# Feed-forward up projection by Strassen's seven block products, with the gated values through DRAM

## The chip, the cores and the metric

The kernel runs on one core of a Trainium2 chip. The metric is the device time of one execution in microseconds (us), as the median over runs.

## What is computed

A backbone of two layers works on 1024 latent tokens and 256 context tokens of 1024 features, all in float32. Each layer has a mixer (attention, long convolution, linear attention), an output projection, and a feed-forward part with 2816 hidden features:

```python
def swiglu(u, w1, w3, w2):
    return (jax.nn.silu(u @ w1) * (u @ w3)) @ w2

h_lat = h_lat + g1_l * merge_heads(attn_l, hy_out_l, gla_out_l, r_l, out_norm_g, w_out)
h_lat = h_lat + g2_l * swiglu(modulate(rms_norm(h_lat, norm2_g), sh2_l, sc2_l), ffn_w1, ffn_w3, ffn_w2)
if update_ctx:      # layer 0 only
    h_ctx = h_ctx + g1_c * merge_heads(...)
    h_ctx = h_ctx + g2_c * swiglu(modulate(rms_norm(h_ctx, norm2_g), sh2_c, sc2_c), ffn_w1, ffn_w3, ffn_w2)
```

The modulation vectors (`sh2`, `sc2`, `g2` and their like) are products of a conditioning vector with `ada_w`. In layer 1 the context is no longer updated.

## The kernel before

Features lie on partitions and tokens along the free axis. Tokens come in blocks `BLK`: block 0 and block 1 of 512 latent tokens, block 2 of 256 context tokens. Every float32 operand of a matmul is split into a high and a low part (`split`: ScalarE copies the rounded high part, GpSimd subtracts it and writes the low part), and `mm3` makes one product of three matmuls: high by high, high by low, low by high. All matmuls of the program have the line of `mm`, L175; every low part has the line of `lo`, L187; every high part that is a plain copy has L421.

`phase34` holds the part that changes. In order: the output projection `w_out` (block 0, then blocks 1 and 2, the residual `h` staying in SBUF); norm 2 (`square` sums the squares, `spread` brings the reciprocal root of each token to all partitions through a matmul with `ones`, `norm_u` scales, shifts and splits into `u`); then the feed-forward part over 22 chunks of 128 hidden features, taken in pairs `m0`, `m0 + 1`. For each chunk `hidden(m, b)` makes the two products of `u` with `ffn_w1` and `ffn_w3` for a block (2 x 8 x 3 matmuls), gates them (L1497, L1498) and splits the gated value into `g` (L1499, L187), which stays in SBUF. After the two chunks of a pair, the down projection adds eight products for each block to `h` (L1537), six matmuls each. The last pair also makes the squares for the norm that follows.

`ada_dve` makes half a modulation vector on VectorE (16 instructions, L327 and L329, over rows of `ada_w` streamed into the tile `nsq`); `ada_next` starts the next of them and closes the one before with four wide and four narrow float32 matmuls.

Order: the program is written in program order, and a planner then fixes each engine's order ahead of the run. It issues on each engine, as it expects times, the ready instruction that stands earliest in program order. In the run each engine goes through its fixed list and stops at the first instruction whose operands are not there. All DMAs named here are issued by SyncE (SP), also in a fixed list. Tiles of one tag share a few buffers; a new tile of the tag waits until the last reader of the old one is done. Pools that are closed give their room to pools opened later, and each new tile there waits for the readers of the old tiles that lay at its place (`reuse_waits="tile"`).

## Time and profile before

| | |
|---|---|
| runs | 3711.64, 3715.42, 3720.87 us; median 3715.42 us |
| the profiled execution, first to last instruction | 3712.2 us |
| PE busy | 3563.2 us, 96% of the span, 17903 matmuls |
| VectorE (DVE) busy | 2014.1 us, 54% |
| GpSimd (POOL) busy | 1353.5 us, 36% |
| ScalarE (ACT) busy | 1088.0 us, 29% |
| feed-forward part of layer 0 | about 1102 to 2072 us of the span |
| feed-forward part of layer 1 | about 2964 us to the end |
| DMA | 310.63 MB, 84 GB/s over the span |

The profile is one execution. Its own time is given as its span of 3712.2 us; no separate time of that execution stands around it, and the median of the runs lies 3.2 us above it. Times in its rows are microseconds from the start of the span; PE is TensorE's matmuls, PEld its weight loads. A row's idle time names the engine that ended it.

### The profile page before, as it was taken

What the parts mean: (1) busy time and instruction counts of PE and PEld (TensorE: products, weight loads), DVE (VectorE), ACT (ScalarE), POOL (GpSimd) and SP (SyncE); (2) the same over time, 40 slices, a digit from 0 to 9 for tenths busy, and PEclk for the clock granted to TensorE, in tenths of its full rate; (3) what the DMA queues carried; (4) which work ended last, traced back from release to release, by engine and by line L of the source; (5) the groups of instructions that cost most, each with busy time, mean ns of one, the idle gap of its engine ahead of it and who ended that gap; (6) DMA issues with size and microseconds to landing.
All of it is one profiled execution on the core that took longest, in us unless ns stands there. A gap on an engine that the chain in (4) does not pass through costs nothing.

```text
span 3712.2 us, 46254 instructions
## 1 busy us (share of the span) xinstructions
PE 3563.2 (96%) x17903; PEld 2693.5 (73%) x17903; DVE 2014.1 (54%) x3271; ACT 1088.0 (29%) x1956; POOL 1353.5 (36%) x960
## 2 busy tenths in 40 slices
PE   8999899999999999999999899899999999999999
PEld 4789845445677888888888688865445788888887
DVE  6755667863677665644223773757753533223233
ACT  4243233553422111111111333333554421111112
POOL 2424564664333111111111541656764542221221
PEclk9999999999999999999999899999999999999999
DMA  9333311120633323321111333411112421111111
GB/s 329 99 124 123 120 33 43 56 81 20 212 110 99 95 80 89 90 66 54 49 35 46 107 111 116 150 49 42 35 70 71 139 63 51 40 57 46 52 40 57
DMA packets 275804, 310.63 MB, mean 84 GB/s; under 512 B 18680, under 2 KB 205727, under 8 KB 274304
## 3 DMA queue, kind: packets, MB, share of 16 engines
q1 hardware_dynamic: 269279, 287.75, 24.6%
q0 software_dynamic: 2560, 13.89, 1.0%
q10 hardware_dynamic: 3744, 6.03, 0.4%
q8 instruction: 140, 2.29, 0.3%
q14 instruction: 81, 0.66, 0.1%
HBM read 245.75 MB, written 61.87 MB: 83 GB/s over the span
## 4 chain that ended last, share of the span: by engine, by line
PE 75%; DVE 11%; POOL 4%; issue 3%; DMA 3%; ACT 1%; SPq 0%; DVEq 0%; POOLq 0%; ACTq 0%
PE ps L175 74%; PE ps L184 1%; POOL hss L928 1%; DMA nsq<-in_ada_w 1%; POOL hl L187 1%; DVE acc L329 1%; DVE mx L1032 1%; DVE sg L1138 1%; DMA yr<-y_d 0%; DVE h L1537 0%; POOL hy L936 0%; DVE sg L1150 0%; DVE sg L1151 0%; DVE nacc L365 0%; DVE hx L930 0%
## 5 line engine op out<-in xcount | busy, mean ns | idle before, releaser
L175 PE MATMUL ps<-u,hl 128*128 128x512 f32 (+1 forms) x6504 | 1384.4, 372 | 20.6 <-DVE u L403 6.2
L175 PEld LDWEIGHTS ps<-u,hl 128*128 128x128 f32 x6504 | 1136.3, 190 | 252.5 <-issue 14.9
L187 POOL TENSOR_TENSOR hl<-raw,hl 128x1024 fp32r<-128x1024 f32 x148 | 366.5, 2479 | 944.3 <-ACT hl L421 924.5
L175 PE MATMUL ps<-g,w 128*128 128x512 f32 (+1 forms) x2688 | 556.6, 367 | 10.0 <-DVE h L1537 3.4
L175 PEld LDWEIGHTS ps<-g,w 128*128 128x128 f32 x2688 | 466.6, 190 | 95.5 <-DVE h L1537 5.4
L1068 POOL TENSOR_TENSOR ac<-ac,p 128x512 f32<-128x512 f32 x256 | 354.7, 1394 | 159.4 <-ACT p L1057 158.8
L1498 DVE TENSOR_TENSOR s<-ps,s 128x512 f32<-128x512 f32 (+1 forms) x110 | 70.0, 637 | 614.7 <-PE ps L175 597.3
L1537 DVE SCALAR_TENSOR_TENSOR h<-ps,mod,h 128x512 f32<-128x512 f32 (+1 forms) x448 | 303.5, 687 | 181.8 <-PE ps L175 181.6
L175 PE MATMUL ps<-p,V 128*64 128x512 f32 x672 | 309.8, 607 | 4.7 <-ACT p L1057 2.5
L187 POOL TENSOR_TENSOR w<-raw,w 128x1024 fp32r<-128x1024 f32 x44 | 109.0, 2477 | 500.0 <-ACT w L421 499.9
L1032 DVE TENSOR_REDUCE mx<-ps 128x1 f32<-128x512 f32 (+1 forms) x400 | 221.0, 587 | 120.8 <-PE ps L175 119.8
L1057 ACT ACTIVATE p<-ps 128x512 f32<-128x512 f32 (+1 forms) x336 | 194.6, 586 | 286.8 <-PE ps L175 277.7
L175 PEld LDWEIGHTS ps<-Q,K 65*128 65x128 f32 (+1 forms) x672 | 105.0, 191 | 222.2 <-issue 209.8
L421 ACT CAST hl<-raw 128x1024 fp32r<-128x1024 f32 x148 | 154.9, 1049 | 303.9 <-PE ps L175 151.5
L329 DVE SCALAR_TENSOR_TENSOR acc<-nsq,silc,acc 128x512 f32<-128x512 f32 x252 | 210.6, 876 | 61.3 <-DMA nsq<-in_ada_w 60.6
L175 PE MATMUL ps<-Q,K 65*128 65x512 f32 (+1 forms) x672 | 242.2, 442 | 1.2 <-ACT p L1057 1.1
L175 PE MATMUL ps<-y,hl 128*128 128x512 f32 (+1 forms) x960 | 213.8, 381 | 13.2 <-DVE y L187 6.1
L175 PEld LDWEIGHTS ps<-y,hl 128*128 128x128 f32 x960 | 170.8, 194 | 59.3 <-DVE y L187 8.2
L421 ACT CAST w<-raw 128x1024 fp32r<-128x1024 f32 x44 | 46.2, 1051 | 491.8 <-PE ps L175 443.2
L175 PE MATMUL ps<-my,dft 128*128 128x256 f32 (+1 forms) x1176 | 166.8, 294 | 10.3 <-DVE my L187 9.7
L1499 ACT CAST g<-s 128x512 fp32r<-128x512 f32 (+1 forms) x110 | 63.3, 576 | 385.2 <-DVE s L1498 385.2
L175 PEld LDWEIGHTS ps<-my,dft 128*128 128x128 f32 x1176 | 159.1, 203 | 20.6 <-DVE my L187 13.7
(265 smaller groups left out, 4129.2 us busy)
## 6 DMA issues: line engine op xcount, KB each, us to landing
raw<-in_ffn_w SPq DMA_DIRECT2D x132, 512.0 KB
nsq<-in_ada_w SPq DMA_DIRECT2D x144, 256.0 KB
raw<-in_w_in SPq DMA_DIRECT2D x36, 512.0 KB
raw<-in_w_out SPq DMA_DIRECT2D x32, 512.0 KB
ada<-in_ada_w SPq DMA_DIRECT2D x24, 512.0 KB
h_d<-h SPq DMA_DIRECT2D x32, 256.0 KB
dft<-in_c_dft POOLq DMA_DIRECT2D x8, 1024.0 KB, 7.2
qd<-qT_d SPq DMA_DIRECT2D x64, 128.0 KB
```

The costliest lines, as they stand in the source:

```text
L175: self.nc.tensor.matmul(out, w, x, start=start, stop=stop)
L184: self.nc.tensor.transpose(out, in_, self.ident[:n, :n])
L187: eng.tensor_tensor(out=out, in0=x, in1=hi.bitcast(F32), op=ALU.subtract)
L329: nc.vector.scalar_tensor_tensor(out=acc[w], in0=raw, scalar=s, in1=acc[w], op0=ALU.mult, op1=ALU.add)
L421: self.nc.scalar.copy(hi, raw)
L928: nc.gpsimd.tensor_tensor(out=ss, in0=ss, in1=self.mh[:, :nh], op=ALU.pow)
L1032: nc.vector.tensor_reduce(out=mx[:, j, i:i + 1], in_=pm, op=ALU.max, axis=AX.X)
L1057: nc.scalar.activation(p, st, AF.Exp)
L1068: nc.gpsimd.tensor_tensor(out=acc[j], in0=x, in1=ps[j], op=ALU.add)
L1498: nc.vector.tensor_tensor(out=s, in0=p3, in1=s, op=ALU.mult)
L1499: nc.scalar.copy(gs[m][:, 0, o:o + n], s)
L1537: nc.vector.scalar_tensor_tensor(out=h, in0=ps, scalar=self.mod[l][:, 40 + k, w:w + 1], in1=h, op0=ALU.mult, op1=ALU.add)
```

## The change

The up projection of the 1024 latent tokens is no longer made chunk by chunk. Two chunks of hidden features by two halves of the 1024 input features form a 2 x 2 matrix of weight blocks (`A11` to `A22`), and two halves of the features by the two token blocks form a 2 x 2 matrix of activations (`B11` to `B22`). The method `up` takes, for each pair of chunks and each of the two weight matrices, seven block products of four `mm3` each instead of eight. Four of the seven use sums of weight blocks (`S1` to `S4`, VectorE), which are split on the fly; four use sums of activation blocks (`T1` to `T4`), which the new method `norm_sums` makes once for each layer in place of block 1's norm, on VectorE, ScalarE and GpSimd. Partial sums are copied out of PSUM between products and the same bank is added to further. The context tokens (layer 0) keep their eight products a weight matrix and chunk.

The gated values of all 22 chunks go to DRAM (`g_d`), and the down projection becomes a second phase that loads them back, splits them (ScalarE and GpSimd) and uses them. `h` leaves SBUF for the duration of `up`: `w_out` stores each piece to `h_d`, and the down phase loads it again. The `ada` work is spread over the pairs of `up`.

```diff
+        usc = self.pool("us", 1, reuse_waits="tile")
+        us = usc.__enter__()
+        B = {n: self.t(us, [P, 2, 4, 512], F32R, n) for n in ("T3", "T4", "B22", "T1", "T2")}
+        B["B11"], B["B21"] = u[0][:, :, 0:4], u[0][:, :, 4:8]
+        for b in blks[1:]:
+            for k in range(KC):
+                r[b] = self.square(self.h[b], k, BLK[b][1], aux, r.get(b))
+            if b == 2:
+                norm2(2, us)
+            else:
+                self.norm_sums(B, a[:, :, 0], self.mod[l][:, 24:32, 0], self.spread(r[0], 512, aux), self.spread(r[1], 512, aux), aux)
+        self.hpool.__exit__(None, None, None)
+        with self.pool("up", 1, side="right", reuse_waits="tile") as wp:
+            self.up(l, B, u.get(2), wp, ada_next, 0 if last else 14)
+        usc.__exit__(None, None, None)
...
+            for b in blks:
+                o, n = BLK[b]
                 for k in range(KC):
+                    nc.sync.dma_start(out=self.h[b][:, k, :], in_=self.h_d[k][:, o:o + n])
...
             for m0 in range(0, NHC, 2):
+                for m in (m0, m0 + 1):
+                    raw = self.t((self.wp, wp)[m % 2], [P, KC, P], F32, "raw", 1)
                     nc.sync.dma_start(out=raw.rearrange("p a b -> p (a b)"), in_=A["ffn_w2"][l][m * P:(m + 1) * P, :])
+                    if m % 3 < 2:
+                        w2s[m] = self.hl[:, m % 3 * 2048:m % 3 * 2048 + 2048].rearrange("p (s k c) -> p s k c", s=2, k=KC)
+                    else:
+                        w2s[m] = self.t(wp, [P, 2, KC, P], F32R, "w2", 1)
                     self.split(raw, w2s[m][:, 0], w2s[m][:, 1])
+                    raw = self.t(gp, [P, nt], F32, "graw", 2 if last else 1)
+                    nc.sync.dma_start(out=raw, in_=self.g_d[m][:, :nt])
+                    gs[m] = self.t(gp, [P, 2, nt], F32R, "g", 3)
+                    self.split(raw, gs[m][:, 0], gs[m][:, 1])
...
+    def norm_sums(self, B, scale, shift, r0, r1, tp):
+        def block(b, k, r):
+            x = self.t(tp, [P, 512], F32, ("s", "acc")[b], 2)
+            nc.vector.scalar_tensor_tensor(out=x, in0=self.h[b][:, k, :], scalar=scale[:, k:k + 1], in1=r, op0=ALU.mult, op1=ALU.mult)
+            nc.scalar.activation(x, x, AF.Identity, bias=shift[:, k:k + 1])
+            return x
+
+        def out(name, k, x, eng):
+            self.split(x, B[name][:, 0, k], B[name][:, 1, k], eng)
+
+        for k in range(4):
+            b12, b11 = block(1, k, r1), block(0, k, r0)
+            nc.gpsimd.tensor_tensor(out=b11, in0=b12, in1=b11, op=ALU.subtract)
+            out("T1", k, b11, nc.vector)
+            b22 = block(1, k + 4, r1)
+            nc.gpsimd.tensor_tensor(out=b12, in0=b22, in1=b12, op=ALU.subtract)
+            out("T3", k, b12, nc.gpsimd)
+            out("B22", k, b22, nc.vector)
+            b21 = block(0, k + 4, r0)
+            nc.gpsimd.tensor_tensor(out=b11, in0=b22, in1=b11, op=ALU.subtract)
+            out("T2", k, b11, nc.vector)
+            nc.gpsimd.tensor_tensor(out=b21, in0=b21, in1=b11, op=ALU.subtract)
+            out("T4", k, b21, nc.gpsimd)
+
+    def up(self, l, B, uc, wp, ada_next, nada):
+        nc, A = self.nc, self.A
+        self.roles((6,), (7,), (0,), (1,), (2,), (3,), (4, 5))
+        self.cyc = (6,)
+        extra = 2 if uc is not None else 5
+        nring = 0
+        def ring():
+            nonlocal nring
+            i = nring % (4 + extra)
+            nring += 1
+            if i < 4:
+                return self.hl[:, i * 1024:(i + 1) * 1024].rearrange("p (s k c) -> p s k c", s=2, k=4)
+            return self.t(wp, [P, 2, 4, P], F32R, "hs", extra)
+        def parts(a):
+            x = ring()
+            self.split(a, x[:, 0], x[:, 1])
+            return x
+        def tile(n=512, tag="c", bufs=6):
+            return self.t(wp, [P, 512], F32, tag, bufs)[:, :n]
+        def product(ps, a, b, start, more=False):
+            for k in range(4):
+                self.mm3(ps, (a[:, 0, k], a[:, 1, k]), (b[:, 0, k], b[:, 1, k]), start and k == 0, k == 3, skip_group_check=True)
+        def store(m, b, g):
+            o, n = BLK[b]
+            nc.sync.dma_start(out=self.g_d[m][:, o:o + n], in_=g)
+        def gated(m, b, x, y):
+            nc.scalar.activation(x, x, AF.Silu)
+            nc.vector.tensor_tensor(out=x, in0=x, in1=y, op=ALU.mult)
+            store(m, b, x)
+        for p in range(0, NHC, 2):
+            W = []
+            for src in (A["ffn_w1"], A["ffn_w3"]):
+                raws = []
+                for i in range(2):
+                    raw = self.t((self.wp, wp)[min(len(W) + i, 1)], [P, KC, P], F32, "raw", 3 if len(W) + i else 1)
+                    nc.sync.dma_start(out=raw, in_=src[l][:, (p + i) * P:(p + i + 1) * P].rearrange("(k p) c -> p k c", p=P))
+                    raws.append(raw)
+                W.append({"A11": raws[0][:, 0:4], "A12": raws[0][:, 4:8], "A21": raws[1][:, 0:4], "A22": raws[1][:, 4:8]})
+            def summed(w, out, x, y, op):
+                z = tile(512, "S", 4).rearrange("p (k c) -> p k c", k=4)
+                nc.vector.tensor_tensor(out=z, in0=W[w][x], in1=W[w][y], op=op)
+                W[w][out] = z
+            a, d, s1, s2, s5 = ([None, None] for _ in range(5))
+            hl = [{}, {}]
+            for w in range(2):
+                bk = self.ps(3 * w + 1)
+                hl[w]["A12"] = parts(W[w]["A12"])
+                product(bk, hl[w]["A12"], B["B21"], True)
+                hl[w]["A11"] = parts(W[w]["A11"])
+                a[w] = self.ps(3 * w)
+                product(a[w], hl[w]["A11"], B["B11"], True)
+                s1[w] = tile()
+                nc.scalar.copy(s1[w], a[w])
+                nc.vector.tensor_tensor(out=s1[w], in0=bk, in1=s1[w], op=ALU.add)
+            gated(p, 0, s1[0], s1[1])
+            def context(m, x, y):
+                if uc is None:
+                    return
+                ps = []
+                for w in range(2):
+                    ps.append(self.ps()[:, :NCTX])
+                    for k in range(KC):
+                        v = hl[w][x if k < 4 else y]
+                        self.mm3(ps[w], (v[:, 0, k % 4], v[:, 1, k % 4]), (uc[:, 0, k], uc[:, 1, k]), k == 0, k == KC - 1)
+                g = tile(NCTX)
+                nc.scalar.activation(g, ps[0], AF.Silu)
+                nc.vector.tensor_tensor(out=g, in0=ps[1], in1=g, op=ALU.mult)
+                store(m, 2, g)
+            context(p, "A11", "A12")
+            for w in range(2):
+                summed(w, "S1", "A21", "A22", ALU.add)
+                d[w] = self.ps(3 * w + 2)
+                product(d[w], parts(W[w]["S1"]), B["T1"], True)
+                s5[w] = tile()
+                nc.scalar.copy(s5[w], d[w])
+            for w in range(2):
+                summed(w, "S2", "S1", "A11", ALU.subtract)
+                product(a[w], parts(W[w]["S2"]), B["T2"], False)
+                s2[w] = tile()
+                nc.scalar.copy(s2[w], a[w])
+            for w in range(2):
+                summed(w, "S4", "A12", "S2", ALU.subtract)
+                product(d[w], parts(W[w]["S4"]), B["B22"], False)
+                nc.vector.tensor_tensor(out=s2[w], in0=d[w], in1=s2[w], op=ALU.add)
+            gated(p, 1, s2[0], s2[1])
+            for w in range(2):
+                summed(w, "S3", "A11", "A21", ALU.subtract)
+                product(a[w], parts(W[w]["S3"]), B["T3"], False)
+                nc.vector.tensor_tensor(out=s5[w], in0=a[w], in1=s5[w], op=ALU.add)
+            gated(p + 1, 1, s5[0], s5[1])
+            for w in range(2):
+                hl[w]["A22"] = parts(W[w]["A22"])
+                product(a[w], hl[w]["A22"], B["T4"], False)
+            g = tile()
+            nc.scalar.activation(g, a[0], AF.Silu)
+            nc.vector.tensor_tensor(out=g, in0=a[1], in1=g, op=ALU.mult)
+            store(p + 1, 0, g)
+            if uc is not None:
+                for w in range(2):
+                    hl[w]["A21"] = parts(W[w]["A21"])
+                context(p + 1, "A21", "A22")
+            for _ in range(2 if p < 6 else 1 if nada else 0):
+                ada_next()
...
     def w_out(self, l, blks, ys, yp):
...
+                nc.sync.dma_start(out=self.h_d[m][:, BLK[b][0]:BLK[b][0] + n], in_=h)
```

## Rows read from the trace of the kernel before

**Rows 1.** The page: busy time of PE, then the chain that ended last, by engine.

```profile
PE 3563.2 (96%) x17903; PEld 2693.5 (73%) x17903; DVE 2014.1 (54%) x3271; ACT 1088.0 (29%) x1956; POOL 1353.5 (36%) x960
...
PE 75%; DVE 11%; POOL 4%; issue 3%; DMA 3%; ACT 1%; SPq 0%; DVEq 0%; POOLq 0%; ACTq 0%
```

**Rows 2.** Stage windows: busy time and instructions of each engine, clock, DMA share, GB/s.

```profile
1232.00:1822.00 590.00, 590.00 (x3066) 496.44 (x3065) 311.60 (x432) 91.41 (x135) 102.53 (x42) 1.00 0.25 75
...
2985.00:3690.00 705.00, 703.44 (x3160) 584.35 (x3160) 223.22 (x283) 125.72 (x170) 158.63 (x69) 1.00 0.16 48
```

**Rows 3.** Groups by shape, 2985 to 3690 us: busy time, mean ns, idle before.

```profile
L175 PE MATMUL ps<-u,hl 128*128 128x512 f32 x2033 | 463.1, 389 | 0.2 <-POOL u L187 0.2
...
L1537 DVE SCALAR_TENSOR_TENSOR h<-ps,mod,h 128x512 f32<-128x512 f32 x168 | 124.9, 749 | 80.5 <-PE ps L175 80.5
L187 POOL TENSOR_TENSOR hl<-raw,hl 128x1024 fp32r<-128x1024 f32 x41 | 98.5, 2405 | 310.1 <-ACT hl L421 310.1
...
L421 ACT CAST hl<-raw 128x1024 fp32r<-128x1024 f32 x41 | 43.1, 1052 | 127.5 <-issue 70.1 <-PE ps L175 55.7 <-DMA raw<-in_ffn_w 1.7
```

**Rows 4.** Groups by shape, 1232 to 1822 us: narrow matmuls, those of ada.

```profile
L175 PE MATMUL ps<-u,hl 128*128 128x256 f32 x672 | 83.9, 283 | 0.0
...
L175 PE MATMUL ps<-acc,ones 128*64 128x512 f32 x44 | 16.1, 618 | 0.0
```

**Rows 5.** Windows of the tile hl alone, at both starts of the feed-forward part.

```profile
1102.00:1143.00 41.00, 30.33 (x108) 21.80 (x106) 2.07 (x2) 5.18 (x2) 0.83 0.21 61
...
2964.00:2985.30 21.30, 19.45 (x82) 14.96 (x81) 2.11 (x2) 5.19 (x2) 1.00 0.41 121
```

**Rows 6.** Timeline at both starts: block 1's root spread, its first scaled chunk.

```profile
1119.57 1.02 PE L175 MATMUL ps<-nsq,ones 128*128 128x512 f32 x2
...
2979.46 0.75 DVE L397 SCALAR_TENSOR_TENSOR s<-h,nsc,ps 128x512 f32<-128x512 f32 x1 [4.66 <-PE ps L175]
...
2985.30 15.75 PE L175 MATMUL ps<-u,hl 128*128 128x512 f32 x68 [0.17 <-POOL u L187]
```

**Rows 7.** Timeline of one norm, layer 1: scale, shift, high copy, low part.

```profile
2946.17 0.74 DVE L397 SCALAR_TENSOR_TENSOR acc<-h,nsc,ps 128x512 f32<-128x512 f32 x1
2946.28 0.73 ACT L402 ACTIVATE u<-s,mod 128x512 fp32r<-128x512 f32 x1 [0.68 <-DVE s L397]
...
2950.00 1.30 POOL L187 TENSOR_TENSOR u<-acc,u 128x512 fp32r<-128x512 f32 x1
2950.44 0.61 ACT L421 CAST u<-acc 128x512 fp32r<-128x512 f32 x1
```

**Rows 8.** Timeline: VectorE subtractions or sums of 512 columns, alone and beside GpSimd.

```profile
1417.96 1.42 DVE L329 SCALAR_TENSOR_TENSOR acc<-nsq,silc,acc 128x512 f32<-128x512 f32 x2 [0.60 <-DMA nsq<-in_ada_w]
...
1419.29 0.68 DVE L187 TENSOR_TENSOR g<-s,g 128x512 fp32r<-128x512 f32 x1
...
1419.89 8.36 DVE L329 SCALAR_TENSOR_TENSOR acc<-nsq,silc,acc 128x512 f32<-128x512 f32 x6
1419.94 2.95 POOL L187 TENSOR_TENSOR hl<-raw,hl 128x1024 fp32r<-128x1024 f32 x1 [27.31 <-ACT hl L421]
...
1423.98 2.40 POOL L187 TENSOR_TENSOR hl<-raw,hl 128x1024 fp32r<-128x1024 f32 x1 [1.09 <-ACT hl L421]
```

**Rows 9.** Windows of the start of layer 0's output projection (columns as in rows 2).

```profile
964.00:968.00 4.00, 1.44 (x3) 1.16 (x4) 4.00 (x9) 1.97 (x5) 0.63 (x1) 0.58 0.96 289
968.00:972.00 4.00, 4.00 (x12) 3.04 (x10) 4.00 (x6) 2.28 (x3) 2.58 (x1) 0.57 0.87 269
...
990.00:996.00 6.00, 6.00 (x26) 4.32 (x24) 3.55 (x6) 2.22 (x3) 2.39 (x1) 1.00 1.09 353
```

**Rows 10.** Landing of DMAs that write or read the DRAM tensor y_d (from its tile view).

```profile
DMA to landing us min/median/max: 2.0/3.7/6.2
```

More of the change, by code (lines that the diff above doesn't have):

```diff
@@ L171, in act_table, with mm, mm3 @@
         self.epoch.__enter__()
-    def mm(self, out, w, x, start, stop):
-        self.nc.tensor.matmul(out, w, x, start=start, stop=stop)
-    def mm3(self, out, w, x, start, stop):
-        self.mm(out, w[0], x[0], start, False)
-        self.mm(out, w[0], x[1], False, False)
-        self.mm(out, w[1], x[0], False, stop)
+    def mm(self, out, w, x, start, stop, **kw):
+        self.nc.tensor.matmul(out, w, x, start=start, stop=stop, **kw)
+    def mm3(self, out, w, x, start, stop, **kw):
+        self.mm(out, w[0], x[0], start, False, **kw)
+        self.mm(out, w[0], x[1], False, False, **kw)
+        self.mm(out, w[1], x[0], False, stop, **kw)
     def tr(self, out, in_, n=P):
@@ L1456, in phase34 @@
             yc.__exit__(None, None, None)
-        with ExitStack() as es:
-            self.upc = self.pool("u", reuse_waits="tile")
-            up = self.upc.__enter__()
-            if last:
-                es.push(self.upc)
-            wp = es.enter_context(self.pool("w4", 1, reuse_waits="tile"))
-            weights = {}
-            def load(m):
-                c = slice(m * P, (m + 1) * P)
-                ws = []
-                for i, src in enumerate((A["ffn_w1"], A["ffn_w3"])):
-                    j = 2 * m + i
-                    ws.append(self.load_w(src[l][:, c], wp=wp if j % 3 == 2 else None, raws=wp if i else None))
-                weights[m] = ws
-            load(0)
-            for b in blks[1:]:
+        nt = NLAT if last else NTOK
@@ new lines, in phase34 @@
+        usc = self.pool("us", 1, reuse_waits="tile")
+        us = usc.__enter__()
+        B = {n: self.t(us, [P, 2, 4, 512], F32R, n) for n in ("T3", "T4", "B22", "T1", "T2")}
+        B["B11"], B["B21"] = u[0][:, :, 0:4], u[0][:, :, 4:8]
+        if not last:
+            ada = [(l, 5, i) for i in range(2)] + [(l + 1, p, i) for p in range(6) for i in range(2)]
+        for b in blks[1:]:
[5 more added lines that the diff above has]
+                self.norm_sums(B, a[:, :, 0], self.mod[l][:, 24:32, 0], self.spread(r[0], 512, aux), self.spread(r[1], 512, aux), aux)
@@ L1502, in phase34 @@
             for m0 in range(0, NHC, 2):
                 end = m0 == NHC - 2
-                for m in range(m0, m0 + 2):
-                    if m not in weights:
-                        load(m)
-                    ws[m] = weights.pop(m)
-                    gs[m] = self.t(gp, [P, 2, nt], F32R, "g")
-                    raw = self.t(wp, [P, KC, P], F32, "raw", 1)
+                w2s, gs = {}, {}
+                for m in (m0, m0 + 1):
+                    raw = self.t((self.wp, wp)[m % 2], [P, KC, P], F32, "raw", 1)
@@ L1526, in phase34 @@
                     w, r = 0 if b < 2 else 1, None
-                    if end and not last:
-                        hidden(NHC - 1, b)
-                        if norm1:
+                    for k in range(KC):
+                        if k == 2 and norm1:
                             self.norm1(l + 1, *norm1, up)
-                    for k in range(KC):
+                            norm1 = None
                         ps = self.ps()[:, :n]
@@ L1544, in phase34 @@
                         norm1 = b, self.spread(r, n, aux)
-                for _ in range(2 if m0 < 8 else 1):
+                if m0 < 8:
                     ada_next()
```

40 lines of the change are left out of this document (14 added, 26 removed).

## The prediction

> **What bounds the kernel now.** I read the page first, then the chain, then windows over the two feed-forward parts, then groups by shape, then the timeline at the places where the change cuts in. The page says that PE is busy for 96% of the span and the chain runs through PE for 75% of it [rows 1]: time is saved by giving PE less to do, and lost wherever PE is made to stand. The windows sharpen this: from 1232 to 1822 us PE is busy for 590.0 of 590 us, in layer 1 from 2985 to 3690 us for 703.4 of 705, at full clock [rows 2]. There the other engines wait for PE. So each matmul taken out is worth its full length, 463.1 / 2033 = 0.228 us for 512 columns [rows 3] and 83.9 / 672 = 0.125 us for 256 [rows 4], and each new stop costs its full length. All that the change can lose is in its seams: the start of the up phase, the passage to the down phase, and the joints between pairs there.
>
> **Products.** A pair of chunks took 2 chunks x 2 weights x 2 blocks x 24 = 192 wide matmuls for the latent tokens; seven products of 12 for two weights are 168. 24 fewer, times 11 pairs, times 2 layers, is 528, times 0.228 us: **-120 us**. Context and down matmuls stay. Inside a pair I charge nothing. Each product lasts 12 x 0.228 = 2.7 us and needs one split of 512 columns: 0.61 us on ScalarE, 1.30 on GpSimd [rows 7]. GpSimd's 14 splits take 18 of the 38 us of PE in layer 1, 16 take 21 of 50 in layer 0 (with 96 narrow matmuls), and the ring of nine or six places lets them run ahead. A bank that is copied out is used again only after at least one other product, 2.7 us, against a copy of some 0.7. Without that cover each of 308 products would wait; the point is priced below. Stores of gated values wait in SP's list, with the next pair's weight loads behind them, but those have about 20 us of room.
>
> VectorE is the nearest to its limit, in layer 0's first three pairs, which carry two `ada` halves each. Its instructions that read and write SBUF stretch beside GpSimd: six sums took 8.36 us, against 1.42 for two alone, while two GpSimd subtractions ran [rows 8]. If the two exclude each other, such a pair needs 21 on GpSimd, 11 x 0.68 = 7.5 for sums and gates and 32 x 0.71 = 22.7 for `ada`: 51 us, against PE's 38.3 + 12.0 + about 3.8 for `ada`'s wide and narrow matmuls (16.1 / 44 = 0.37 us a wide one [rows 4]) = 54. Covered, barely: **0**, between -5 (layer 0's present first pair stands a few us for `ada` too) and +10.
>
> **The start of the up phase.** Today PE goes from the output projection into `hidden` of block 0, whose `u` has long been made, while block 1's norm runs. It does 108 matmuls (some eight of them narrow) from 1102 to 1143 us, and 82 from 2964.0 to 2985.3 [rows 5], and then never stops. After the change only the four products on `B11` and `B21` (48 matmuls, 10.9 us) can run before the `T` sums. Those need block 1's root, which comes at about 1120 and 2979.5 us [rows 6].
>
> `norm_sums` then goes through four steps. A step has on GpSimd four subtractions and two low parts, 6 x 1.30 = 7.8 us, but the temporaries have two buffers a block, and one chain returns to the same buffer: first subtraction 1.3; its high copy 0.6; its low part on VectorE, shut out by GpSimd's second subtraction, to 3.3; T3's low part and B22's take their turns, to 5.3; third subtraction, 6.6; high copy, 7.3; its low part, shut out again by the fourth subtraction, 8.6; then the buffer is free for scale 0.74 and shift 0.73 [rows 7], with handovers 10.3 us. So T1 is whole after 3 x 10.3 + 2.3 + 3.3 = 36 us, T4 after 43. In layer 1 PE goes on at 36. In layer 0 the ring's last two places lie where `h` of block 2 lay, which that block's norm reads after `norm_sums`, and the second weight's raw tiles lie over block 0's `h`, read until the last step: PE goes on at about 47.
>
> What is lost is what PE would have done by then. Layer 0, by 1167 us: 100 x 0.228 + 8 x 0.125 + 24.0 of unbroken work = 47.8, less 10.9 = 36.9. Layer 1, by 3015: 82 x 0.228 + 29.7 = 48.4, less 10.9 = 37.5. PE comes back at the lower of its two clock levels, 1.2 GHz: after short stops the granted clock was 0.57 to 0.58 over 8 us [rows 9]; I estimate 3 us a restart. Sum **+80 us**. Lower end 62: the steps go at GpSimd's 7.8 us. Upper end 100: two weight splits push into every step.
>
> The exclusion weighs here. Rows 8 show it for low parts and sums; what a subtraction of two plain float32 tiles does, which the step is full of, they don't. By the Trainium skill ("SBUF — State Buffer", Terms) VectorE and GpSimd share a pair of ports held by one of them for a whole instruction, and the loser is blocked fully. By that the step is the 10.3 us above; without any exclusion it would be 8.3 and the sum 16 us less; the trace's six sums agree with it roughly, 4.1 us lost beside 5.35 of GpSimd.
>
> **The passage to the down phase.** The first `ffn_w2` halves lie in the ring, the last product's weights at the same place; the first `g` buffers lie over the temporaries of the last gated value. In layer 1 that is: gate 0.7, store 3.7 (landings of such DMAs took 2.0 to 6.2, median 3.7 [rows 10]), high copy 1.05, low part 2.4 [rows 3] = 8 us of standing PE. In layer 0 the single `graw` lies over the end of block 2's `u`, read to the last context product: load about 5, copy 1.3, low part 3.0 for 1280 columns = 9.3, and the second chunk through the same buffer another 9.3, with 18 matmuls (4.1) between: 14.5. Sum **+22**, from 12 (landings of 2.0) to 31 (6.2).
>
> **The joints between pairs.** `w2` and `g` have three buffers for two chunks a pair, so the second chunk of each pair waits for the first chunk of the pair before, until its last matmul. Then: high copy 1.05, low part of `w2` 2.4, low part of `g` 2.4 (3.0 in layer 0), 5.2 to 5.9 us after the joint. Meanwhile PE can do the first chunk's matmuls in six banks, 18 x 0.228 = 4.1, and six high-by-high ones, 1.4. If the planner orders it like that, a joint costs 0.1 us; if it takes GpSimd for faster, it places the second chunk too early and PE stands in its fixed order, up to 5.5. No row shows which. I take 1.4, a quarter of the way, because the list follows readiness: 20 joints, **+28**, from 2 to 110. VectorE's additions to `h`, 0.75 us each 1.37, are no limit [rows 3].
>
> **The rest.** Stores in `w_out` add 5.2 MB. In layer 0 the DMA engines are full at its start (share 1.09 at 353 GB/s [rows 9]); 2.1 MB cost 6 us there at most, half hidden: **+3**, 0 to 8. Reloading `h` is behind six banks of matmuls: 0. At layer 0's end the next norm loses the cover of `hidden`, but VectorE and GpSimd set that end already: 0.
>
> Sum: -120 + 80 + 22 + 28 + 0 + 3 = +13. The profiled execution's 3712 becomes 3725; the median of the runs stands 3.2 us above it, so I predict **3728 us**, 0.3% slower. Differences under 0.3% (11 us) can't be told from none here.
>
> **Rivals.**
> - *The start closes early.* The planner brings T1 of later steps forward, or buffers come free sooner, and PE resumes 20 us earlier a layer: 3688. For it: T1 alone needs only four subtractions. Against: two buffers, and a list that serves program order. It decides once 12 us a layer are saved: the whole is then faster.
> - *The joints are hidden.* 0.1 us each instead of 1.4: 3702, on the edge between same and faster. For it: 5.5 us of matmuls against 5.2 to 5.9 of splits.
> - *The joints are bare.* 5.5 us each: 3810.
> - *The products don't come at PE's rate.* If banks read between products, or weight splits late beside GpSimd's other work, hold each of 308 products for 0.2 us, 62 us go: 3790; at 0.39 the change saves nothing. Against: GpSimd half idle and 2.7 us of cover.
>
> **Chances.** Forecast 0.42, with its own range 3705 to 3765: 0.27 slower, 0.15 same. Early start 0.20, faster. Hidden joints 0.18, half faster, half same. Bare joints 0.10 and held products 0.10, slower. Together faster 0.29, same 0.24, slower 0.47. The range must reach to the early start and to held products: 3675 to 3795 leaves out the bare joints and the tails of the others.
>
> **What would show it.** Right: windows of about 40 us at both starts with PE busy for a quarter; steps of some 10 us in GpSimd's subtractions; PE full through the up phase, pairs of 38 us in layer 1; PE empty for 8 to 15 us at each passage; a gap of 1 to 2 us every 22 us in layer 1's down phase, released by low parts on GpSimd. Wrong: PE busy through the start, PE stops inside pairs, joints without gaps or with 5 us. The prediction fails most easily by the planner's order, which the trace of before shows only for other work.

## The result, and the profile after

The changed kernel takes 3775.6 us (median of 4 runs, 3763.74 to 3782.99), the kernel before 3717.37 (4 runs beside it): ratio 1.0158, 95% interval 1.0134 to 1.0182. It is slower, as forecast, but by 57 us between the two profiled executions (span 3769.4 against 3712.2) where the forecast was 13.

The page of the changed kernel, busy time and chain by engine, answers to [rows 1]:

```profile
PE 3474.4 (92%) x17379; PEld 2599.1 (69%) x17379; DVE 2210.2 (59%) x3509; ACT 1286.0 (34%) x2320; POOL 1751.5 (46%) x1278
...
PE 36%; issue 6%; DVE 4%; POOL 4%; DMA 2%; ACT 1%; SPq 0%; POOLq 0%; DVEq 0%; ACTq 0%
```

PE has 89 us less to do and the kernel takes 57 us more: it stands 146 us longer. Windows of the changed kernel (columns as in [rows 2]) over the stages: layer 0's start, up phase, passage and end; layer 1's start, up phase, passage and down phase.

```profile
1111.20:1181.00 69.80, 19.89 (x74) 14.21 (x74) 52.11 (x77) 36.01 (x66) 50.45 (x41) 0.61 0.15 43
1181.00:1757.00 576.00, 564.44 (x2952) 472.03 (x2952) 346.43 (x439) 177.44 (x313) 250.64 (x175) 0.99 0.37 111
1757.00:1797.00 40.00, 11.70 (x41) 8.38 (x42) 15.50 (x20) 4.53 (x4) 11.39 (x4) 0.66 0.76 258
2103.90:2156.70 52.80, 33.94 (x88) 23.13 (x89) 37.79 (x67) 21.92 (x42) 31.11 (x31) 0.68 0.24 75
3006.00:3058.00 52.00, 11.82 (x44) 7.97 (x43) 33.73 (x43) 26.26 (x43) 36.98 (x27) 0.61 0.13 35
3058.00:3480.80 422.80, 421.64 (x1818) 342.61 (x1818) 170.32 (x194) 146.74 (x256) 203.10 (x153) 1.00 0.26 80
3480.80:3515.30 34.50, 18.16 (x69) 14.68 (x70) 8.05 (x12) 6.28 (x6) 16.95 (x14) 0.75 0.72 251
3515.30:3740.00 224.70, 222.64 (x999) 182.65 (x998) 118.39 (x168) 43.19 (x48) 91.57 (x39) 1.00 0.26 80
```

Four windows with PE about half empty or emptier stand out: two starts, two passages. A busy share alone misleads, though, since a slow matmul counts as busy. So I count in each stage the matmuls of 512 and 256 columns, take 0.2268 and 0.120 us for one (the period in the kernel before, at full clock), and call the rest of the stage lost:

| stage | lost before, us | lost after, us | difference |
|---|---|---|---|
| products, 2 x 264 matmuls fewer | | | -119.8 |
| starts, layer 0 / layer 1 | 18.3 / 3.1 | 59.9 / 44.9 | +83.4 |
| passages | none | 30.7 / 18.9 | +49.6 |
| up and down phases between | 38.3 / 9.7 | 51.2 / 22.4 | +25.6 |
| layer 0's end | 28.2 | 38.7 | +10.5 |
| output projections, length | 138.8 / 101.2 | 148.9 / 98.1 | +7.0 |
| output's end, layer 1 | | | +2 |

The sum is +58, the spans differ by 57.2. What PE waited for in the changed kernel, in layer 0 from 1111.2 to 2156.7 us (engine and tile waited for: sum, times, longest), and in layer 1 from 3006 us on:

```profile
PE ps L175 <- DVE s L1554: 33.8, 1, 33.8
PE ps L175 <- ACT g L422: 26.9, 2, 25.0
PE ps L175 <- DVE acc L398: 11.3, 2, 6.0
PE ps L175 <- DVE c L1680: 8.8, 4, 3.7
PE ps L175 <- POOL g L187: 7.3, 10, 1.5
...
PE ps L175 <- ACT hs L422: 36.6, 1, 36.6
PE ps L175 <- ACT g L422: 16.4, 1, 16.4
```

Two single stops of 34 and 37 us are the starts; the two of 25.0 and 16.4 us for the high copy of the first gated values are the passages. Of the ten short ones for the low part of `g`, nine (5.8 us together) are joints and the longest, 1.5 us, lies in the passage; layer 1 has no such joint. The four stops for `c` are an addition of VectorE (L1680) in the first pairs of layer 0's up phase. Of the two for `acc`, the one of 6.0 us belongs to block 2's norm at layer 0's start, and the one of 5.3 us to the next norm at layer 0's end.

The timeline of layer 1's start, which answers to [rows 6] (engine, line, operation; first number the start): the root's spread, GpSimd's first subtraction of a step, VectorE's low part beside it, the same subtraction of the second and fourth step, the last low part of T1, PE's return.

```profile
3016.30 1.10 PE L175 MATMUL ps<-nsq,ones 128*128 128x512 f32 x2 [2.35 <-DVE nsq L386]
...
3019.01 1.27 POOL L1563 TENSOR_TENSOR s<-acc,s 128x512 f32<-128x512 f32 x1 [3.77 <-ACT acc L1555]
3020.36 1.73 POOL L1566 TENSOR_TENSOR acc<-acc,acc 128x512 f32<-128x512 f32 x1
...
3020.97 1.67 DVE L187 TENSOR_TENSOR T<-s,T 128x512 fp32r<-128x512 f32 x1
...
3028.98 1.71 POOL L1563 TENSOR_TENSOR s<-acc,s 128x512 f32<-128x512 f32 x1
...
3048.87 1.71 POOL L1563 TENSOR_TENSOR s<-acc,s 128x512 f32<-128x512 f32 x1
...
3051.98 0.68 DVE L187 TENSOR_TENSOR T<-s,T 128x512 fp32r<-128x512 f32 x1
...
3053.97 1.22 PE L175 MATMUL ps<-T,hs 128*128 128x512 f32 x2 [36.58 <-ACT hs L422]
```

The steps are (3048.87 - 3019.01) / 3 = 9.95 us apart, and T1 is whole at 3052.66, 36.4 us after the spread. VectorE's low part, 0.68 us alone, takes 1.67 when GpSimd is subtracting.

Layer 0's start looks alike, but it ends otherwise. The root's spread, two loads for `ada` in SP's list, the spread of block 2's root, the first context products, and the first product with a sum:

```profile
1126.07 1.62 PE L175 MATMUL ps<-nsq,ones 128*128 128x512 f32 x2 [2.08 <-DVE nsq L386]
1134.22 34.34 SPq L324 DMA_DIRECT2D nsq<-in_ada_w  x2
1166.97 1.22 PE L175 MATMUL ps<-nsq,ones 128*128 128x256 f32 x2 [4.46 <-DVE nsq L386]
1174.18 4.66 PE L175 MATMUL ps<-u,hl 128*128 128x256 f32 x24 [5.99 <-DVE acc L398]
1178.91 0.73 PE L175 MATMUL ps<-T,hs 128*128 128x512 f32 x2
```

T1 is whole at 1163.8, 37.7 us after its spread, but PE uses it only at 1178.9. Two things are late besides. In PE's list the context products stand ahead, and they wait for block 2's norm. And the second of the two loads for `ada` goes into a buffer of `nsq` and stands in SP's list until block 2's spread is done; the other three weight tiles of the first pair are loaded behind it, at 1168.6, and VectorE makes the first weight sum at 1177.5. Both end at about the same time.

Layer 1's passage in the same view:

```profile
3481.61 0.32 SPq L1608 DMA_DIRECT2D g_d<-c  x1
3481.98 7.58 SPq L1488 DMA_DIRECT2D h<-h_d  x14
...
3489.96 0.32 SPq L1509 DMA_DIRECT2D graw<-g_d  x1
...
3496.04 1.04 ACT L422 CAST g<-graw 128x1024 fp32r<-128x1024 f32 x1 [14.13 <-DMA graw<-g_d]
...
3497.14 3.35 PE L175 MATMUL ps<-g,hl 128*128 128x512 f32 x7 [16.36 <-ACT g L422]
```

SP issues the last gated store, then 14 reloads of `h` for 7.6 us, and only then the load of the gated values that PE stands for.

### The profile page after: what moved, and what is told of

It reads as the page before. It is cut to its first block, busy times and chain, and to the rows that moved or that the text cites. A ratio compares the mean times of both kernels' runs of the same rounds, so it can differ in the third digit from the quotient of the medians.

```text
span 3769.4 us, 47538 instructions
## 1 busy us (share of the span) xinstructions
PE 3474.4 (92%) x17379; PEld 2599.1 (69%) x17379; DVE 2210.2 (59%) x3509; ACT 1286.0 (34%) x2320; POOL 1751.5 (46%) x1278
## 4 chain that ended last, share of the span: by engine, by line
PE 36%; issue 6%; DVE 4%; POOL 4%; DMA 2%; ACT 1%; SPq 0%; POOLq 0%; DVEq 0%; ACTq 0%
PE ps L175 35%; POOL g L187 1%; POOL hl L187 1%; PE ps L184 1%; DMA graw<-g_d 1%; POOL hss L929 0%; DMA h<-h_d 0%; DMA raw<-in_w_out 0%; DVE mx L1033 0%; DVE sg L1139 0%; DVE nacc L366 0%; DMA raw<-in_ffn_w 0%; DVE S L1628 0%; POOL u L187 0%; POOL hy L937 0%
## 5 line engine op out<-in xcount | busy, mean ns | idle before, releaser
L187 POOL TENSOR_TENSOR hl<-raw,hl 128x1024 fp32r<-128x1024 f32 (+1 forms) x180 | 350.3, 1949 | 548.5 <-ACT hl L422 527.5
L175 PE MATMUL ps<-u,hl 128*128 128x512 f32 (+1 forms) x2544 | 531.8, 361 | 35.0 <-DVE acc L398 11.3
L175 PEld LDWEIGHTS ps<-u,hl 128*128 128x128 f32 x2544 | 424.0, 195 | 122.0 <-DVE acc L398 12.7
L175 PE MATMUL ps<-g,hl 128*128 128x512 f32 (+1 forms) x1824 | 416.3, 370 | 48.5 <-ACT g L422 43.3
L175 PEld LDWEIGHTS ps<-g,hl 128*128 128x128 f32 x1824 | 321.6, 190 | 112.6 <-ACT g L422 44.3
L175 PE MATMUL ps<-T,hl 128*128 128x512 f32 x1152 | 274.7, 393 | 10.0 <-DVE c L1680 10.0
L175 PE MATMUL ps<-T,hs 128*128 128x512 f32 x960 | 234.5, 399 | 37.9 <-ACT hs L422 36.6
L175 PEld LDWEIGHTS ps<-T,hl 128*128 128x128 f32 x1152 | 216.6, 189 | 56.2 <-DVE c L1680 11.2
L175 PEld LDWEIGHTS ps<-T,hs 128*128 128x128 f32 x960 | 181.0, 190 | 82.2 <-ACT hs L422 37.7
L175 PE MATMUL ps<-g,w 128*128 128x512 f32 (+1 forms) x864 | 212.7, 366 | 2.1 <-POOL g L187 2.1
```

The lines of the kernel that those rows point to most:

```text
L175: self.nc.tensor.matmul(out, w, x, start=start, stop=stop, **kw)
L187: eng.tensor_tensor(out=out, in0=x, in1=hi.bitcast(F32), op=ALU.subtract)
```

## The experiments

Each run is the changed kernel with one edit, or, where it is said, with edits of earlier runs; ratios are to the kernel before, with 95% intervals. Passage first.

**Run 1, the reload of `h` behind the first pair's loads** in the order of the program; ratio 1.0101 (1.0084 to 1.0118).

```
-            for b in blks: ...  dma_start(out=self.h[b][:, k, :], in_=self.h_d[k][:, o:o + n])
             wp = es.enter_context(self.pool("w4", ...
...
+                if m0 == 0:
+                    for b in blks: ...  dma_start(out=self.h[b][:, k, :], in_=self.h_d[k][:, o:o + n])
```

> The residual h is read back after the loads of the first down pair instead of ahead of them, in both layers; nothing else differs from the changed kernel. My theory: in the changed kernel SyncE's list issues 16 to 24 reloads of h (7.6 us of issuing in layer 1, longer in layer 0, where loads of ada weights stand between them) ahead of the first load of gated values, so PE waits 16.4 us at layer 1's passage and 25.0 + 3.5 us at layer 0's. With the loads first, layer 1 should wait some 8 us and layer 0 some 14.5, the amounts that I forecast; the span falls by about 20 us, to 3749. Rival: the first load of gated values waits for its room, freed by the last gated tile's store, and the reloads ahead of it cost nothing: the waits stay at 16 and 28 us and the span at 3769.

The waits of this run at the two passages:

```profile
PE ps L175 <- ACT g L422: 15.8, 2, 9.2
...
PE ps L175 <- ACT g L422: 10.1, 1, 10.1
```

They were 26.9 and 16.4: the place in SP's list is worth 11.1 and 6.3 us. The span of the profiled execution fell by only 8.7, to 3760.7, but that execution is the longest of run 1's four (3762.47 us; the others took 3753.03 to 3755.35), and 6.5 us of it are lost before the output projection of layer 0 begins (968.8 us against 962.3). The medians fell by 21 us, from 3775.6 to 3754.3, which agrees with the 17.4 us of waiting. What is left is the wait that I had forecast: gate, store, load, copy.

**Runs 2 and 3, the stores of `h` in the output projection.** In layer 0 that projection takes 10 us longer than before. Run 2 writes the stores after the projection, but they were still issued inside it, so it tells nothing (1.0143, 1.0128 to 1.0159; projection 147.8 us). Run 3 was to hold them back by a dependency (1.0124, 1.0107 to 1.0142).

```
+        with self.tc.issue_after(self.lasth.ins):
+            for b in blks: ...  dma_start(out=self.h_d[k][:, o:o + n], in_=self.h[b][:, k, :])
```

> The 40 stores of h are all issued after the output projection instead of inside it. My theory: in layer 0 the DMA engines are full during the output projection, and the stores delay its loads: its 148.9 us become about 140, as before the change (138.8), the stores pass in the stretch where PE stands for the block sums, and the span falls by 7 to 10 us. In layer 1, whose output projection got no longer, nothing changes. Rival: the lengthening comes from where the adaLN sums fall on VectorE, and the stores are innocent: the output projection stays at 148 us, and the late stores push the first pair's weights back, so that the span stays or grows by up to 8 us.

> The stores of h are now truly held back until the last addition of the output projection (in the kernel with late stores the planner had put them forward again, so that it told nothing). Theory A, the stores delay the loads of layer 0's output projection: its 148 us become about 140, the span falls by 7 to 10. Theory B, they are innocent: the output projection stays at 148 us, and the span changes by less than 5, or grows where the held stores keep the room of h from the first pair's weights.

In run 3 the projection takes 148.5 us, but the stores were not held back: in its trace SP issues the first two of layer 0's 24 at 992.55 us and 18 of them before 1094, while the projection runs from 970.9 to 1119.7. Run 3 tells as little as run 2, and whether the stores lengthen the projection stays untested.

**Run 4, two of the four subtractions of a step on VectorE** (T1's and T2's); 1.0151 (1.0135 to 1.0168).

```
-            nc.gpsimd.tensor_tensor(out=b11, in0=b12, in1=b11, op=ALU.subtract)
+            nc.vector.tensor_tensor(out=b11, in0=b12, in1=b11, op=ALU.subtract)
```

> Two of the four subtractions of each step of the block sums (those for T1 and T2) go to VectorE; GpSimd keeps two subtractions and two low parts. A step took 9.95 us. Theory A, VectorE's instructions with two SBUF inputs and GpSimd's exclude each other: 6 x 1.27 + 3 x 0.68 = 9.7 explains the step, and now 4 x 1.27 + 5 x 0.68 = 8.5: PE stands some 5 us less in each layer, the span falls by 9 to 10. Theory B, GpSimd's own six instructions set the step with the handovers: now GpSimd has 5.1 us and VectorE 4 x 0.74 + 5 x 0.68 = 6.4, the step is about 6.5 to 7, PE stands 12 to 14 us less a layer, the span falls by some 25.

The step went from 9.95 to 8.72 us (first subtractions at 3027.25, 3035.97 and 3044.68). Its timeline, the fourth step and PE's return:

```profile
3044.68 0.68 DVE L1563 TENSOR_TENSOR s<-acc,s 128x512 f32<-128x512 f32 x1
...
3049.88 3.42 DVE L1628 TENSOR_TENSOR S<-raw 128x512 f32<-128x512 f32 x2
...
3052.33 1.22 PE L175 MATMUL ps<-T,hs 128*128 128x512 f32 x2 [36.18 <-ACT hs L422]
```

T1 was whole 33.2 us after the spread, 3 us earlier, and PE still came back after 36.2 us of idling: the sum of weights S1, which takes its turn on VectorE after the steps, was late next. In layer 0 the stop fell from 33.8 to 31.0. The step is what held T1, but not all that holds PE: by its median, 3771.3 us, run 4 can't be told from the changed kernel.

**Run 5, layer 1's weights only in the ring's four places in `hl`,** the room of the other five kept; 1.013 (1.0115 to 1.0145). Groups by shape had shown the up phase's matmuls unequal. In the changed kernel, 3058 to 3480 us (count, busy time, mean ns):

```profile
L175 PE MATMUL ps<-T,hs 128*128 128x512 f32 x574 | 139.9, 399 | 0.9 <-POOL hs L187 0.9
L175 PE MATMUL ps<-T,hl 128*128 128x512 f32 x478 | 112.1, 390 | 1.1 <-DVE c L1680 1.1
L175 PE MATMUL ps<-u,hs 128*128 128x512 f32 x288 | 70.0, 396 | 0.0
L175 PE MATMUL ps<-u,hl 128*128 128x512 f32 x212 | 50.8, 390 | 0.0
```

```
-            i = nring % (4 + extra)
+            i = nring % (4 + (extra if uc is not None else 0))
```

> In layer 1 the split weights of the products take turns in the four places of hl alone, not in nine; the room of the other five stays reserved, so that every other tile keeps its place. In the changed kernel a matmul whose weights lie in one of the five places hs comes 231 to 236 ns after the one before, one whose weights lie in hl 227, whatever the moving operand. Theory A, the place of the weights sets it: all of layer 1's products go at 227 ns, the 422.8 us of the up phase become about 415, and the span falls by 7. Theory B, it comes from what else goes on beside the product (splits, sums, other engines' traffic), the period of these matmuls stays at 231 to 236 in part, and the phase keeps its length; in either case four places could run dry, which would show as PE waiting for low parts on GpSimd, and I expect under 3 us of that.

The same view of run 5:

```profile
L175 PE MATMUL ps<-T,hl 128*128 128x512 f32 x1054 | 249.9, 391 | 0.9 <-POOL hl L187 0.9
L175 PE MATMUL ps<-u,hl 128*128 128x512 f32 x501 | 120.7, 390 | 0.0
```

From the first to the last T matmul of layer 1 it is 417.9 us instead of 426.4, and the span is 7.2 shorter. Weights in `hs` cost PE about 7 ns a matmul, for whichever moving operand.

**Run 6, T1 made first** (on run 5's ring); 1.0096 (1.0081 to 1.0112).

```
-            nc.gpsimd.tensor_tensor(out=b11, in0=b12, in1=b11, op=ALU.subtract)
-            out("T1", k, b11, nc.vector)
...
+            tt(nc.vector, t1[k], b12[k], half(u0, 0, k))
+            tt(nc.vector, t1[k], t1[k], half(u0, 1, k))
+            out("T1", k, t1[k], nc.vector)
```

> On top of the ring of four: the block sums are made in another order and from other sources. T1 of all four chunks comes first, then T2 and B22, then T3 and T4; block 0 is read from the two halves of its normed tokens instead of from h, so that the raw weights and first sums may lie over block 0's h at once; low parts and subtractions are nearly all on VectorE; the first pair of layer 0 does its context products last. Theory A, PE stands at the start of the up phase because the first product that needs sums needs T1 whole, and this order finished it only 36 us after the root: T1 comes after 4 x 2.8 = 11 to 12 us, T2 and B22 after another 13, PE stands in two pieces of about 13 and 7 us; some 20 us less in each layer, and the span falls from the ring of four's 3762 to about 3724. Theory B, PE is held by something else as well (first weight sums, weight splits, the list order): PE still stands more than 30 us in a layer, and the span falls by less than 20.

That is Theory B: the span is 3755.3, 6.9 us under run 5. In layer 1 PE stood for 32.9 us all the same: the first pair's weights were loaded only at 3037.24, because their room now lay over the temporaries of the block sums. In layer 0 they came at 1154.96, behind the loads for `ada` in SP's list, PE stood for 23.4 and 18.1 us, and from the end of the output projection on the layer took 7 us more than in run 5. T1 had been the last of several late things, not the only one.

**Run 7, the down phase on the low side:** weights, gated values and sums there, `h` on the high side, with run 1's order; 1.0044 (1.0027 to 1.0061).

```
-            wp = es.enter_context(self.pool("w4", 1, side="right", reuse_waits="tile"))
-            gp = es.enter_context(self.pool("g", 2, side="right", reuse_waits="tile"))
+            wp = es.enter_context(self.pool("w4", 1, reuse_waits="tile"))
+            gp = es.enter_context(self.pool("g", 2, reuse_waits="tile"))
...
```

> The down phase changes alone: w2, g and their raw tiles lie on the left, over the block sums that are free early, and h on the right; the reloads of h come behind the first pair's loads; the first w2 has a place of its own, so that it can be split before the last product. Theory A, the passage is a matter of room and of list order: PE stands 0 to 3 us in layer 1 and 3 to 6 in layer 0 (was 16.4 and 28.5), and the matmuls of the down phase, whose operands now lie low as before the change, come at 227 ns instead of 229 to 236; the span falls by 30 to 40, to about 3733. Theory B, the reload of h sets the passage: it needs the last gated store and then 4 to 5 MB at some 330 GB/s, 12 to 16 us, so that after six banks (8 us) PE stands again for 5 to 10 us; the span falls by no more than after moving the reloads alone, some 20.

Its waits at layer 0's and layer 1's passage:

```profile
PE ps L175 <- ACT g L422: 7.3, 2, 6.6
...
PE ps L175 <- ACT g L422: 2.7, 2, 1.5
```

The span is 3733.4, as expected, and 36 us under the changed kernel. The first gated values no longer lie over the last gate's temporaries, so they are loaded while PE still multiplies.

**Run 8, runs 7 and 5 together;** 1.003 (1.0018 to 1.0041).

> The change with two edits together: the down phase's weights, gated values and sums on the low side with h reloaded behind the first pair's loads (span 3733.4 alone, 36 us under the kernel after) and layer 1's up phase drawing its weights from the ring of four at the low addresses (3762.2 alone, 7.2 under). Theory A, each takes away a stall of its own (a queue's order and a matmul period): they add, span 3733.4 - 7.2 to 8.5 = 3725 to 3726, layer 1's seven products from the first T matmul to the last in 418 us. Rival, they share a gain (what the low addresses give in one phase is lost at the other's passage): span 3731 or more.

Span 3724.0, layer 1 from the first to the last T matmul 417.7 us: the two add. What is left against the kernel before, 12 us, is less than the two starts cost.

**Run 9, the first pair ahead of the sums** (on run 8): the weights of the first pair in place of block 0's `h`, its products on block 0 and the split S1 before the block sums, T1 first, nearly all subtractions on VectorE; 1.0046 (1.0033 to 1.0059).

```
+        pre = self.early(l, B, hp)       # loads, splits, B21 and B11 products, split S1
...
+                tt(nc.vector, t1[k], b12[k], half(u0, 0, k))
+                tt(nc.vector, t1[k], t1[k], half(u0, 1, k))
+                last = out("T1", k, t1[k], nc.vector)
```

> The kernel of the run above with the start of the up phase put in another order in both layers: the products of the first pair and the split first sums stand ahead of the block sums, T1 is made first from the halves that block 2's root does not touch, then T2 and B22, then T3, T4, and all first subtractions but T4's lie on VectorE, so that the first product can begin when T1 alone is whole. Theory A, the start is held by the sums in a row (the kernel after: first sum matmul 36 us after the root's spread, TensorE idle 33.8 and 36.6 us): T1 is whole 10 to 15 us after the spread, TensorE's longest idle stretch in each layer falls under 20 us, span 3725 - 2 x 20 = 3685, below the kernel before (3712). Rival B, something else arrives as late (the first pair's weights, block 2's norm, SP's loads): idle stays over 25 us in a layer, and the span is 3705 or more.

The timeline of PE in layer 1 of this run:

```profile
3021.20 2.07 PE L175 MATMUL ps<-nsq,ones 128*128 128x512 f32 x2 [2.55 <-DVE nsq L386]
3029.14 1.22 PE L175 MATMUL ps<-T,hl 128*128 128x512 f32 x2 [5.87 <-ACT T L1579]
...
3053.06 1.22 PE L175 MATMUL ps<-T,hl 128*128 128x512 f32 x2 [13.75 <-ACT hl L422]
3060.75 4.60 PE L175 MATMUL ps<-T,hl 128*128 128x512 f32 x12 [6.47 <-POOL hl L187]
```

T1 is whole 12 us after the spread (36.4 in the changed kernel) and its products run; then PE waits 13.8 and 6.5 us for the next weight sums, which stand behind T2's and T3's work on VectorE. Layer 1 from the end of its output projection on takes 5 us less than in run 8. In layer 0 the weight sums come behind the loads for `ada` and block 2's norm as well, PE stands for 32.7 us in one piece, and the layer loses 21 us against run 8. Rival B, then, and in layer 0 worse than that. The 21 us are those of the profiled execution, the longest of run 9's six (3728.8 to 3743.7 us); by the medians the whole kernel lost 4.6 us against run 8.

**Runs 10 and 11, the change in layer 1 alone.** Run 10 is run 8 with layer 0's feed-forward part as in the kernel before. Run 11 has also run 9's start in layer 1, with the second and third weight sums made, and the second split, before the root.

```
-                self.phase34(l)
+                (self.phase34 if l else self.phase34_first)(l)   # phase34_first: that of the kernel before
...
+            nc.vector.tensor_tensor(out=z, in0=z, in1=a11[w], op=ALU.subtract)    # S2, in early()
+            self.split(z, x[:, 0], x[:, 1])
+            nc.vector.tensor_tensor(out=z, in0=a12[w], in1=z, op=ALU.subtract)    # S4
```

> Layer 0's feed-forward part as in the kernel before (no Strassen, no passage), layer 1's as in the run with the low side and the ring of four. Theory A, the two layers' ledgers are separate: layer 0 costs what it does in the kernel before (layer 1's last w_out product at 2964.3, or some 3 us earlier for its shorter layer-1 stretch), layer 1 from there on 740.1 us as in that run, against 747.9 in the kernel before: span 3700 to 3705 against 3712, ratio 0.997 to 0.998. Rival, what layer 1 gains hangs on what layer 0 left (the place of the pools, the order of the loads): layer 1 takes 748 us or more, span 3712 or more.

> The run beside it, with layer 1's start in the order of the run that put the first pair's products ahead, and in addition the first pair's second and third weight sums made and (the second) split before the root, B22 ahead of T2, and T2 ahead of T3 on VectorE. In that run layer 1 was 5 us shorter, and TensorE stood 13.8 us for the second weight sum's high part, 6.5 for its low part, 5.9 for T1, 2.6 for the root. Theory A, the weight sums' place in VectorE's order held the second product: T1 whole 12 us and T2 whole 25 to 27 us after the spread, TensorE's longest stop in the start under 10 us, all stops there under 20 (29.8 in that run), span 3685 to 3694, ratio about 0.994. Rival, T3 and T4 are late next (VectorE and GpSimd take all two-input work in a row for 40 us): the stops move behind T2 and add to 28 or more, span 3697 or more.

Run 10: ratio 0.9981 (0.9968 to 0.9994), span 3707.2; layer 1 from its last output-projection matmul on takes 742.5 us against 747.9 before. Run 11: **0.9939 (0.9921 to 0.9956)**, median 3692.65 us, span 3692.9, faster than both kernels. PE in its layer 1:

```profile
2984.97 2.08 PE L175 MATMUL ps<-nsq,ones 128*128 128x512 f32 x2 [5.20 <-DVE nsq L386]
2992.91 1.22 PE L175 MATMUL ps<-T,hl 128*128 128x512 f32 x2 [5.87 <-ACT T L1736]
2995.27 8.02 PE L175 MATMUL ps<-T,hl 128*128 128x512 f32 x22 [1.14 <-DVE T L1737]
3007.53 5.07 PE L175 MATMUL ps<-T,hl 128*128 128x512 f32 x14 [4.24 <-ACT c L1884]
...
3023.63 6.43 PE L175 MATMUL ps<-T,hl 128*128 128x512 f32 x20 [2.40 <-POOL hl L187]
```

The stop of 36.6 us has become five that add to 18.9, none over 5.9.

## Why the prediction was right in direction and short in size

**The range.** The measured 3775.6 us lies in the range only because its end was put at 3795 to take in the held products, which did not happen; the forecast's own range ended at 3765. That the time fell inside is luck; the sum was some 45 us short.

**Products: right in layer 1.** -120 forecast, -119.8 counted. The up phase of layer 1 shows PE busy for 421.64 of 422.80 us, so products and splits inside a pair cost no stop there; "held products" did not happen. In layer 0 VectorE, put at 0 ("covered, barely", -5 to +10), made PE stand four times in the first pairs, 8.8 us in all.

**The start: right in layer 1 by its mechanism, in layer 0 only in its size.** +80 forecast, +83.4 found; steps of 10.3 us forecast, 9.95 found; T1 36 us after the root, 36.4 found. By the Trainium skill ("SBUF — State Buffer", Terms) the port pair that VectorE and GpSimd share is held for a whole instruction; the trace agrees, with 9.95 us near the 10.3 of that sum and far from 8.3, and run 4's 8.72 agrees as well. One detail was wrong: 24 matmuls ran before the stop in layer 1, not 48. The second weight's tiles were not late there: their loads were issued by 3009.6 us, and the DMA engines were idle from 3016 on; but ScalarE copied their high parts only at 3053.82, behind the block sums in its fixed list. Why the planner put them there stays open. That the loss came out right all the same is in part luck: the 24 missing matmuls cost 5.4 us, and the root came sooner: VectorE first used it 11.4 us after the output projection, 15.2 in the kernel before. And the step was called the whole of the hold. In layer 1 the weight sums stood close behind it, as run 4 showed; in layer 0 PE came back 52.8 us after the spread, not 47, and 15 us after T1 was whole: the context products ahead of it waited for block 2's norm, and the first pair's weights were loaded behind a load for `ada`. The two end together, so the trace does not tell which decides. Runs 6 and 9 met the same loads.

**The passage: the step that failed.** +22 forecast, +49.6 found. The prediction said "Reloading `h` is behind six banks of matmuls: 0". It is, for the sums that need `h`; but its loads stand ahead of the first gated values in SP's list, and I had not counted them as instructions of a queue that the passage goes through. Run 1 took 17.4 us of waiting away by moving them alone. The wait that remained, 15.8 and 10.1 us, is near the 14.5 and 8 of the forecast; most of the rest of the 49.6 is PE's slower matmuls after the stop, at a granted clock of 0.66 and 0.75 in those windows (in layer 1 ten of them came 0.43 us apart). Run 7 took most of the remaining wait away (7.3 and 2.7 us left) with the gated values in another place; it moved `w2`, `h` and the sums as well, so that their place alone did it is argued from its loads, not shown.

**The joints: wrong.** +28 forecast; 5.8 us found, nine stops of 0.6 us on average, all in layer 0. The rival "hidden joints" was the truer one. That the total for the up and down phases came out near 28 all the same (+25.6) is chance: in layer 0, +12.9 with the four stops for VectorE's addition in it; in layer 1, +12.7 without a single joint. There 7 to 8.5 us are the longer matmul period of weights in `hs` (run 5). Of the remainder, the down phase's matmuls with `g` and `w2` on the high side came 229 to 230 ns apart on average, and 227 on the low side in run 7; that run moved several things at once, so its share is argued, not shown.

**Layer 0's end: wrong.** 0 forecast, +10.5 found. The last stretch, for the same 72 wide matmuls, took 52.8 us against 32.5 before, and the stretch ahead of it lost 10 us less: `hidden` of the last chunk, which covered the next norm, is gone, and PE waits for that norm: eleven short stops, 18.9 us together and the longest 5.3, against four and 8.3 us before, at a granted clock of 0.68 against 0.82. I did not test this alone.

**The output projection.** +3 forecast, +7.0 found (+10.1 in layer 0, -3.1 in layer 1). The cause stays open. Runs 2 and 3 left the stores inside it. With layer 0's feed-forward part as before it is 140.2 and 138.7 us (runs 10 and 11), but those runs have neither the stores nor the changed later work in layer 0, so they don't tell the one from the other.

The terms together: 120 us of work saved, 83 lost at the starts, 50 at the passages, 45 elsewhere. Runs 7 and 5 gave back 45 of those; the start could be mended in layer 1, where nothing but the norm competes; the two orders tried in layer 0 (runs 6 and 9) made it worse, with the weights again behind `ada`'s loads.

## What to carry to other kernels

When work is taken from an engine that is 96% busy, the price is paid at the seams: write out, for each seam, every instruction in every queue that the first operand of the next phase passes through, the reloads that nobody waits for included. A product that needs sums of operands should have its first operands, weights as well as tokens, made before the late input arrives, so that only what depends on that input is left in the gap. And a change that pays in one layer need not pay in another: with its seams mended and applied where the queues were free, it gained 0.6%; as it was, in both layers, it lost 1.6%.

## What the runs showed of the hardware that was not expected

The time from one 512-column matmul to the next depends on the tile its weights come from. Of the changed kernel's timeline in the middle of layer 1's up phase, PE (a row is a run of matmuls, its length 0.16 us more than their periods):

```profile
3206.37 5.60 PE L175 MATMUL ps<-T,hl 128*128 128x512 f32 x24
...
3220.37 8.56 PE L175 MATMUL ps<-T,hs 128*128 128x512 f32 x36
...
3231.50 5.60 PE L175 MATMUL ps<-B,hl 128*128 128x512 f32 x24
```

That is (5.60 - 0.16) / 24 = 0.2267 us with weights in `hl`, at the low end of SBUF, and (8.56 - 0.16) / 36 = 0.2333 with weights in `hs`, at the high end. PE counts as busy in both, so no view of waits or busy shares shows it; only counting matmuls does. The Trainium skill ("SBUF — State Buffer", Who interferes with whom) says that TensorE never waits on another engine at SBUF. The rows do not say that it does, but they do say that the tile matters for 3%; whether by the address itself or by what else lies and is written there, no run told apart. A place at the high end alone does not do it: in the changed kernel's down phase of layer 1, weights in `w`, also on the high side, came 229 ns apart on average and most of them 226 to 228.

VectorE and GpSimd shut each other out for subtractions of two SBUF tiles as for low parts, in both directions: GpSimd's took 1.27 us alone and 1.71 to 1.73 beside VectorE's, VectorE's 0.68 and 1.67. With two of four subtractions moved to VectorE a step takes 4 x 1.27 + 5 x 0.68 = 8.5 us if all exclude each other, and 8.72 was measured.
